# The opening of a hybrid attention and DeltaNet layer: modulation products in plain float32 on four column groups, tokens loaded first, squares shared between two engines

## The chip, the cores and the metric

The kernel runs on one NeuronCore of a Trainium2 chip. The metric is the device time of one execution in microseconds. The core has five engines that each work through their own list in order: TensorE (PE in the profile, with its weight loads PEld), VectorE (DVE), ScalarE (ACT), GpSimd (POOL) and SyncE (SP). In this kernel SP does nothing but issue DMA transfers.

## The reference, cut to what matters

One layer mixes 512 latent tokens x and 256 context tokens ctx, each 1024 wide. Everything starts with a modulation: two vectors c and c_ctx give shifts, scales and gates, and the tokens are normed, scaled and shifted before the first projection.

```python
mod_lat = jax.nn.silu(c) @ w_mod + b_mod          # 1024 -> 6144
mod_ctx = jax.nn.silu(c_ctx) @ w_mod + b_mod
sh1, sc1, g1, sh2, sc2, g2 = ... split(mod_lat, 6)
csh1, csc1, ... = split(mod_ctx, 6)
hx = rms_norm(x) * (1.0 + sc1) + sh1
hc = rms_norm(ctx) * (1.0 + csc1) + csh1
... = split_cols(hx @ w_in)                       # attention q, k, v, DeltaNet q, k, v, gates
... = split_cols(hc @ (w_in[:, :CTX_COLS]))
```

After that come grouped-query attention, a bidirectional gated DeltaNet, a gated merge, an output projection and a gated MLP with a short convolution. The change touches only the part that makes sh1, sc1, csh1, csc1 (the first 2048 columns of w_mod), the norms, hx and hc.

## The kernel before, in words

All matrices are float32. A large product is made from two parts of each operand, a high part in the type float32r and the rest (`split`: a copy on ACT, a subtraction on DVE), and three products high x high, high x low, low x high (`mm3`). A product of plain float32 operands appears in the trace as two matmul instructions.

The opening has these pieces, written out as a list of steps in the string `ORD` (L40) that `step` (L580 and after) executes one by one. The order of TensorE's instructions in this part is pinned to that list; the other engines' orders are chosen by a planner from priorities (`sooner`, `first`) and expected ready times.

- Loads. The string `LORD` (L55) gives the order on the SP queue: `x0` is the context (256 tokens), `x1` and `x2` the latent tokens, `w0` to `w7` are the eight halves of the first 2048 columns of w_mod, each 1 MB, `h0` and `h1` the weights of the first two DeltaNet key heads, 0.5 MB each. Tokens and w halves share `WB` (L56) buffers. Behind them on the queue come the rotary tables and the first key weights.
- Norm (L486 to L492). For each of the three token tiles, ACT squares the two groups of 128 tokens with a running sum, the inverse root is one DVE, one POOL instruction, and DVE scales the tokens in place.
- `x0` to `x11` in `ORD` (`x_cols`). Four float32 transposes each, into one of two PSUM banks, and a copy out by ACT or DVE: after twelve of them the tokens stand with channels on partitions.
- `g`, or `a` and `b` for the two halves (`gemv`, L496). One chunk of the modulation: 1024 channels in eight pieces k of 128, times 512 columns (256 of the shift, 256 of the scale), for the two vectors. The weights stream, the vectors are stationary. For the first `FKS` pieces the weights are split by ACT and DVE and multiplied in float32r with both parts of the vectors (four stationary columns), the rest are plain float32 products with two stationary columns. One PSUM bank (`PMB`), and a copy to `mrow` by ACT.
- `m` (`mod_cols`). Four transposes turn the row into columns, and DVE adds the bias and the two partial rows.
- `y` (`modulate`). For two of the eight channel tiles: scale and shift on DVE (latent) and ACT (context), then the split into the operands hxH, hxL, hcH, hcL.
- `p` (`early_proj`), or its halves `q` and `r` for one head each: one channel tile of the first two key heads' projections. It needs `y` of that tile.
- `d` (`warm`): products of zeros that only keep TensorE busy, four for each unit.

After `p7` the kernel goes on with the attention's keys, whose first product is the group `pq<-whi,hcH` in the trace. It does not return to this part.

Of the kernel before, what the change touches and what calls it, by code (L numbers as in the profile page):

```python
# [14 lines left out]
P = 128  # L15
D = 1024
KT = 8
# [17 lines left out]
POOLW = 0  # L35
ND, D0U = 4, 6
KV = 10
GN = ''
FKS = '4466'
# [6 lines left out]
WHB = 3  # L46
PMB = 1
XV, YV = 4, 0
NS = 2
# [29 lines left out]
def hybrid_layer_body(tc, x, ctxt, xT, consts, cols, rows, w_mod1, w_mod2, w_av, w_aq, w_cm, w_pa, w_pd, w_out,  # L79
                      w_up, w_down, outT, dbg=None):  # L80
    nc = tc.nc
    V, A, G, SP = nc.vector, nc.scalar, nc.gpsimd, nc.sync
# [11 lines left out]
    T = Ordered()  # L94
# [14 lines left out]
    def put(i):  # L109
        return tc.keep_in_program_order(i) if strict[0] else i  # L110
# [6 lines left out]
    def tt(out, a, b, op, eng=None):  # L117
        put((eng or V).tensor_tensor(out=out, in0=a, in1=b, op=op))  # L118

    def ts(out, a, s1, op0, s2=None, op1=None, eng=None):  # L120
        if op1 is None:
            (eng or V).tensor_scalar(out=out, in0=a, scalar1=s1, scalar2=None, op0=op0)
        else:
            (eng or V).tensor_scalar(out=out, in0=a, scalar1=s1, scalar2=s2, op0=op0, op1=op1)  # L124
# [4 lines left out]
    def act(out, a, f=AF.Copy, **kw):  # L129
        put(A.activation(out, a, f, **kw))  # L130

    def split(hi, lo, src):
        act(hi, src)
        tt(lo, src, hi, ALU.subtract)
# [6 lines left out]
    def mm(ps, a, b, start=True, stop=True):  # L141
        T.matmul(ps, a, b, start=start, stop=stop)

    with es:
# [23 lines left out]
        ident = cst[:, C_ID:C_ID + 128]  # L168
# [37 lines left out]
        def xbank():  # L206
            return xps.tile([P, 4, P], F32, name="xb", tag="x")
# [44 lines left out]
        hxH = hxp.tile([P, KT, NL], F32R, name="hxH")  # L252
# [191 lines left out]
        with m1_es:  # L444
            m1 = m1_es.enter_context(tc.tile_pool(name="m1", bufs=1))
            mps = m1_es.enter_context(tc.tile_pool(name="mps", bufs=NB, space=PSUM))
            xs = []
            wms = []

            def ordered_load(out, in_):  # L450
                i = SP.dma_start(out, in_)
                if LPIN:
                    tc.keep_in_program_order(i)

            hw = []
            for op in LORD.split():
                i = int(op[1])
                with sooner():
                    if op[0] == "w":
                        wms.append(m1.tile([P, 4, 512], F32, name="wm", tag="in", bufs=WB))  # L460
                        ordered_load(wms[i], w_mod1[i // 2, i % 2])
# [16 lines left out]
            cs = m1.tile([P, 16], F32, name="cs")  # L478
            act(cs, col[:, S_C:S_C + 16], AF.Tanh, scale=0.5)
            stt(cs, cs, 1.0, col[:, S_C:S_C + 16], ALU.add, ALU.mult)  # L480
            ts(cs, cs, 0.5, ALU.mult)
            cs4 = m1.tile([P, KT, 4], F32R, name="cs4")
            split(cs4[:, :, 0:2], cs4[:, :, 2:4], cs.rearrange("p (k two) -> p k two", two=2))
            ss = m1.tile([P, 6], F32, name="ss")
            rs = m1.tile([P, 6], F32, name="rs")
            for i in range(3):  # L486
                for t in range(2):
                    act(hxH[:, 6:8, :].rearrange("p a b -> p (a b)"), xs[i][:, t, :], AF.Square, accum_out=ss[:, 2 * i + t:2 * i + t + 1])
                sl = slice(2 * i, 2 * i + 2)
                rsqrt(rs[:, sl], ss[:, sl], 1.0 / D, EPS)  # L490
                for t in range(2):
                    ts(xs[i][:, t, :], xs[i][:, t, :], rs[:, 2 * i + t:2 * i + t + 1], ALU.mult)  # L492
            m2 = lambda t, o: t[:, o:o + 16].rearrange("p (s k) -> p s k", s=2)
            wsl = lambda k: slice(k * P, k * P + P)

            def gemv(nb, k0=0, k1=KT):  # L496
                if k0 == 0:
                    mpm[nb] = mps.tile([P, 512], F32, name="pm", tag="pm", bufs=PMB)[0:4]
                ps = mpm[nb]
                for k in range(k0, k1):  # L500
                    wm, j = wms[2 * nb + k // 4], k % 2
                    if k >= int(FKS[nb]):
                        mm(ps[0:2], cs[:, 2 * k:2 * k + 2], wm[:, k % 4, :], False, k == KT - 1)
                        continue
                    if j == 0:
                        wmh = m1.tile([P, 2, 512], F32R, name="wmh", tag="wmh", bufs=WHB)
                        wml = m1.tile([P, 2, 512], F32R, name="wml", tag="wml", bufs=WHB)
                        act(wmh, wm[:, k % 4:k % 4 + 2, :])
                        tt(wml, wm[:, k % 4:k % 4 + 2, :], wmh, ALU.subtract, G if k % 4 == 0 and str(nb) in GN else V)
                    mm(ps, cs4[:, k, :], wmh[:, j, :], k == 0, False)  # L510
                    mm(ps[0:2], cs4[:, k, 0:2], wml[:, j, :], False, k == KT - 1)
                if k1 == KT:
                    mrows[nb] = m1.tile([4, 512], F32, name="mrow", tag="mrow", bufs=2)
# [12 lines left out]
            sides = ((hxH, hxL, mod, hx_pair), (hcH, hcL, modc, hc_pair))  # L526
            stash = [[pair(F32) for _ in range(KT // 2)] for pair in (hx_pair, hc_pair)]
# [42 lines left out]
            mrows, mpm = {}, {}  # L570
# [32 lines left out]

            for op in ORD.split():
                step(op[0], int(op[1:]))
# [81 lines left out]
        with kv_es:  # L687
# [716 lines left out]
        for p in range(NP):  # L1404
# [7 lines left out]
            out = (None, gdn_out(0), gdn_out(1), gdn_reload())[p]  # L1412
# [12 lines left out]
        x1 = [x1p.tile([P, NL], F32, name=f"x1_{c}") for c in range(KT)]  # L1425
# [258 lines left out]
```

## Time and profile before

| what | value |
|---|---|
| device time, median of 3 runs | 1252.84 us (1252.52 to 1253.11) |
| span of the profiled execution, first to last instruction | 1246.8 us |
| time of the profiled execution outside its span | not listed on the page; the median above is 6.0 us over the span |
| TensorE busy | 1194.3 us, 96% of the span |
| VectorE, ScalarE, GpSimd busy | 828.6, 613.8, 248.8 us |
| TensorE's mean granted clock | 0.985 |

The profile has these views. The page gives busy times and the costliest groups. The timeline gives one engine's instructions in order: start, length, engine, line, operation, `output<-inputs`, and in brackets how long the engine sat idle before it and what released it. Instructions on a tile have the tile's name without its number, and where a helper records an operation, all have the helper's line (L87 for products, L91 for transposes, L118, L122, L124, L127 for DVE and POOL operations, L130 for ACT). The table of stages gives each engine's busy time and number of instructions between two times, then the granted clock, the DMA share and the rate in GB/s. A length on TensorE includes the pipeline's end, so the distance of two starts is what an instruction occupies.

### The profile page before, as it was taken

To read this page: it belongs to the slowest core of one execution; us is meant where nothing else is said; L and a number is where in the kernel's file an instruction comes from. 1 tells how busy PE (TensorE), PEld (TensorE's weight loads), DVE (VectorE), ACT (ScalarE), POOL (GpSimd) and SP (SyncE) were. 2 spreads that over 40 slices of the span, in tenths; PEclk is the share of its full clock that TensorE was granted. 3 is DMA by queue.
4 is the path that set the end of the run, shared out by engine and by line. 5 is a ranking of instruction groups with operands and counts; after the bars stand their busy time and mean duration, and the time that the engine had idled before them with its cause. 6 is when DMAs were issued, how large, how long until landed. Compare 5 with 4: busy or idle time off the path is not lost.

```text
span 1246.8 us, 20481 instructions
## 1 busy us (share of the span) xinstructions
PE 1194.3 (96%) x7733; PEld 1018.2 (82%) x7733; DVE 828.6 (66%) x1623; ACT 613.8 (49%) x1403; POOL 248.8 (20%) x333
## 2 busy tenths in 40 slices
PE   7999999999999989999999999999999999999996
PEld 4599889888887778788887778789888888888886
DVE  5766767878699757666646687866766755653333
ACT  6634467777565754754634532234544444442321
POOL 0120110010313596596483000000000000000000
PEclk8999999999999999999999999999999999999998
DMA  9412321333536526345335685863344323323331
GB/s 380 144 60 85 92 80 60 119 98 106 199 104 211 165 73 189 111 153 176 118 123 186 225 273 196 302 235 114 103 135 135 125 95 102 101 82 104 93 94 68
DMA packets 67555, 174.98 MB, mean 140 GB/s; under 512 B 7456, under 2 KB 18176, under 8 KB 66048
## 3 DMA queue, kind: packets, MB, share of 16 engines
q1 hardware_dynamic: 67456, 173.67, 41.9%
q8 instruction: 61, 1.00, 0.3%
q14 instruction: 38, 0.31, 0.1%
HBM read 146.85 MB, written 26.79 MB: 139 GB/s over the span
## 4 chain that ended last, share of the span: by engine, by line
PE 52%; DMA 4%; DVE 3%; ACT 2%; POOL 1%; issue 1%; SPq 0%; POOLq 0%; DVEq 0%; ACTq 0%
PE mc L87 33%; PE mb L87 13%; PE pb L87 5%; DMA gt<-atd 1%; DVE wlo L118 1%; DMA M<-gamdr 1%; ACT whi L130 1%; PE pk L87 1%; DMA wl<-in_w_mod_dram 1%; PE pqk L87 0%; POOL NN L118 0%; DMA wraw<-in_w_pa_dram 0%; DMA cw<-in_rows_dram 0%; DMA NN<-gamdr 0%; ACT Gb L130 0%
## 5 line engine op out<-in xcount | busy, mean ns | idle before, releaser
L118 DVE TENSOR_TENSOR wlo<-wraw,whi 128x1024 fp32r<-128x1024 f32 (+1 forms) x153 | 188.0, 1230 | 158.2 <-ACT whi L130 157.7
L130 ACT ACTIVATE whi<-wraw 128x1024 fp32r<-128x1024 f32 (+1 forms) x153 | 159.6, 1044 | 217.0 <-PE mc L87 114.4
L87 PE MATMUL mc<-h,whi 128*128 128x512 f32 (+1 forms) x752 | 219.6, 376 | 0.3 <-ACT whi L130 0.3
L87 PE MATMUL mb<-hxH,whi 128*128 128x512 f32 x384 | 162.3, 423 | 1.7 <-DVE t L127 1.7
L87 PEld LDWEIGHTS mc<-h,whi 128*128 128x128 f32 x752 | 138.0, 188 | 25.8 <-ACT whi L130 0.5
L87 PE MATMUL mb<-hxH,wlo 128*128 128x512 f32 x384 | 152.3, 397 | 0.0
L87 PE MATMUL mb<-hxL,whi 128*128 128x512 f32 x384 | 152.0, 396 | 0.0
L87 PE MATMUL mc<-h,wlo 128*128 128x512 f32 (+1 forms) x376 | 141.3, 376 | 0.5 <-DVE wlo L118 0.5
L87 PE MATMUL mc<-a,whi 128*128 128x512 f32 (+1 forms) x396 | 111.0, 366 | 0.6 <-DVE x L127 0.6
L118 POOL TENSOR_TENSOR rc<-rc,mhalf 128x2 f32<-128x2 f32 x4 | 3.2, 810 | 456.0 <-DVE rc L124 456.0
L87 PEld LDWEIGHTS mb<-hxH,wlo 128*128 128x128 f32 x384 | 73.0, 190 | 16.8
L87 PEld LDWEIGHTS mb<-hxH,whi 128*128 128x128 f32 x384 | 73.4, 191 | 11.9 <-issue 2.1
L87 PEld LDWEIGHTS mc<-h,wlo 128*128 128x128 f32 x376 | 70.8, 188 | 13.8 <-DVE wlo L118 1.0
L87 PEld LDWEIGHTS mc<-a,whi 128*128 128x128 f32 x396 | 71.6, 189 | 12.8 <-DVE x L127 0.8
L87 PEld LDWEIGHTS mb<-hxL,whi 128*128 128x128 f32 x384 | 73.4, 191 | 9.2
L87 PE MATMUL mc<-a,wlo 128*128 128x512 f32 (+1 forms) x198 | 72.3, 365 | 0.0
L127 DVE SCALAR_TENSOR_TENSOR u<-mc,col,u 128x511 f32<-128x511 f32 x88 | 65.3, 746 | 1.4
L118 POOL TENSOR_TENSOR R<-R,prod 128x31 f32<-128x31 f32 (+15 forms) x93 | 58.0, 623 | 6.7
L118 POOL TENSOR_TENSOR prod<-X,R 128x31 f32<-128x31 f32 (+15 forms) x93 | 53.2, 572 | 20.0 <-DVE X L118 13.2
L87 PE MATMUL pq<-whi,hxH 128*128 128x256 f32 (+1 forms) x192 | 55.5, 289 | 0.0
L87 PE MATMUL pq<-wlo,hxH 128*128 128x256 f32 (+1 forms) x192 | 54.3, 283 | 0.1
L87 PE MATMUL pq<-whi,hxL 128*128 128x256 f32 (+1 forms) x192 | 54.2, 282 | 0.0
(329 smaller groups left out, 2737.5 us busy)
## 6 DMA issues: line engine op xcount, KB each, us to landing
wraw<-in_w_cm_dram SPq DMA_DIRECT2D x48, 512.0 KB, 3.6
wraw<-in_w_up_dram SPq DMA_DIRECT2D x44, 512.0 KB, 3.3
wl<-in_w_mod_dram SPq DMA_DIRECT2D x24, 512.0 KB, 4.9
wm<-in_w_mod_dram SPq DMA_DIRECT2D x8, 1024.0 KB, 10.5
wraw<-in_w_down_dram SPq DMA_DIRECT2D x16, 512.0 KB, 3.6
wraw<-in_w_aq_dram SPq DMA_DIRECT2D x10, 512.0 KB, 3.8
M<-gamdr SPq DMA_DIRECT2D x64, 64.0 KB, 4.5
wraw<-in_w_pa_dram SPq DMA_DIRECT2D x8, 512.0 KB, 4.5
```

Of the source, the lines that this page charges most:

```text
L87: i = nc.tensor.matmul(*a, **k)
L118: put((eng or V).tensor_tensor(out=out, in0=a, in1=b, op=op))
L127: V.scalar_tensor_tensor(out=out, in0=a, scalar=s, in1=b, op0=op0, op1=op1)
L130: put(A.activation(out, a, f, **kw))
```

## The change

- `LORD`: the three token tiles are loaded first, then w0, w1, h0, h1, and the other w halves. `WB` goes from 6 to 8 buffers.
- The norm: ACT squares the first group of each token tile and DVE the second.
- `gemv`: no split of the weights. The two vectors stand in a stationary operand of 32 columns, 30 of them zero (`cs32`, cleared by POOL). Piece k is a plain float32 product that writes the 32 PSUM partitions of column group k modulo 4, so that a half (four pieces) addresses the four groups of the array one after another. `mrow` has 128 partitions.
- `mod_cols`: instead of transposes, four float32 products with 128 columns of `mrow` stationary and a selector `sel` (128 x 2) streaming; the selector adds the four groups' rows of each vector. DVE has one addition per vector instead of two.
- `ORD`: all products in halves; the first chunk now comes among and behind the transposes, and one warming step stands before the first turn into columns.

```diff
-ORD = 'd4 g0 x0 x1 x2 x3 m0 x4 x5 x6 x7 x8 a1 x9 x10 x11 y0 b1 p0 m1 y1 p1 g2 p2 m2 y2 p3 g3 q4 m3 y3 r4 p5 p6 p7'
+ORD = 'd4 x0 x1 x2 x3 x4 x5 x6 x7 a0 x8 x9 x10 x11 b0 d1 m0 y0 a1 p0 b1 p1 m1 y1 a2 b2 p2 m2 y2 p3 a3 b3 p4 m3 y3 p5 p6 p7'
...
-LORD = 'w0 w1 x0 x1 x2 w2 w3 h0 h1 w4 w5 w6 w7'
-WB = 6
+LORD = 'x0 x1 x2 w0 w1 h0 h1 w2 w3 w4 w5 w6 w7'
+WB = 8
...
-            ts(cs, cs, 0.5, ALU.mult)
-            cs4 = m1.tile([P, KT, 4], F32R, name="cs4")
-            split(cs4[:, :, 0:2], cs4[:, :, 2:4], cs.rearrange("p (k two) -> p k two", two=2))
+            cs32 = m1.tile([P, KT, 32], F32, name="cs32")
+            G.memset(cs32, 0.0)
+            ts(cs32[:, :, 0:2], cs.rearrange("p (k two) -> p k two", two=2), 0.5, ALU.mult)
+            sel = m1.tile([P, 2], F32, name="sel")
+            V.tensor_reduce(out=sel, in_=ident.rearrange("p (b c) -> p c b", c=32)[:, 0:2, :], axis=AX.X, op=ALU.add)
...
-                for t in range(2):
-                    act(hxH[:, 6:8, :].rearrange("p a b -> p (a b)"), xs[i][:, t, :], AF.Square, accum_out=ss[:, 2 * i + t:2 * i + t + 1])
+                junk = [hxH[:, k:k + 2, :].rearrange("p a b -> p (a b)") for k in (6, 2)]
+                act(junk[0], xs[i][:, 0, :], AF.Square, accum_out=ss[:, 2 * i:2 * i + 1])
+                V.scalar_tensor_tensor(out=junk[1], in0=xs[i][:, 1, :], scalar=1.0, in1=xs[i][:, 1, :], op0=ALU.mult, op1=ALU.mult,
+                                       accum_out=ss[:, 2 * i + 1:2 * i + 2])
...
-                    wm, j = wms[2 * nb + k // 4], k % 2
-                    if k >= int(FKS[nb]):
-                        mm(ps[0:2], cs[:, 2 * k:2 * k + 2], wm[:, k % 4, :], False, k == KT - 1)
-                        continue
-                    if j == 0:
-                        wmh = m1.tile([P, 2, 512], F32R, name="wmh", tag="wmh", bufs=WHB)
-                        wml = m1.tile([P, 2, 512], F32R, name="wml", tag="wml", bufs=WHB)
-                        act(wmh, wm[:, k % 4:k % 4 + 2, :])
-                        tt(wml, wm[:, k % 4:k % 4 + 2, :], wmh, ALU.subtract, G if k % 4 == 0 and str(nb) in GN else V)
-                    mm(ps, cs4[:, k, :], wmh[:, j, :], k == 0, False)
-                    mm(ps[0:2], cs4[:, k, 0:2], wml[:, j, :], False, k == KT - 1)
+                    q = slice(32 * (k % 4), 32 * (k % 4) + 32)
+                    mm(ps[q], cs32[:, k, :], wms[2 * nb + k // 4][:, k % 4, :], k < 4, k >= 4)
...
-                pst = xbank()[:, 0, 0:16].rearrange("p (a b) -> p a b", b=4)
+                pst = xbank()[:, 0, 0:8].rearrange("p (a b) -> p a b", b=2)
                 for i in range(4):
-                    T.transpose(pst[:, i, :], mrow[:, i * P:(i + 1) * P], ident[0:4, 0:4])
+                    mm(pst[:, i, :], mrow[:, i * P:(i + 1) * P], sel)
...
                     tt(m2(md, 0)[:, :, ks], p4[:, :, :, j], m2(col, S_BMOD)[:, :, ks], ALU.add)
-                    tt(m2(md, 0)[:, :, ks], p4[:, :, :, 2 + j], m2(md, 0)[:, :, ks], ALU.add)
```

More of the change, by code (lines that the diff above doesn't have):

```diff
@@ L37 @@
 KV = 10
-GN = ''
-FKS = '4466'
-ORD = 'd4 g0 x0 x1 x2 x3 m0 x4 x5 x6 x7 x8 a1 x9 x10 x11 y0 b1 p0 m1 y1 p1 g2 p2 m2 y2 p3 g3 q4 m3 y3 r4 p5 p6 p7'
+ORD = 'd4 x0 x1 x2 x3 x4 x5 x6 x7 a0 x8 x9 x10 x11 b0 d1 m0 y0 a1 p0 b1 p1 m1 y1 a2 b2 p2 m2 y2 p3 a3 b3 p4 m3 y3 p5 p6 p7'
 RK = 1.0
@@ L45 @@
 TG = 1
-WHB = 3
 PMB = 1
@@ L497, in gemv @@
                 if k0 == 0:
-                    mpm[nb] = mps.tile([P, 512], F32, name="pm", tag="pm", bufs=PMB)[0:4]
+                    mpm[nb] = mps.tile([P, 512], F32, name="pm", tag="pm", bufs=PMB)
                 ps = mpm[nb]
                 for k in range(k0, k1):
-                    wm, j = wms[2 * nb + k // 4], k % 2
-                    if k >= int(FKS[nb]):
-                        mm(ps[0:2], cs[:, 2 * k:2 * k + 2], wm[:, k % 4, :], False, k == KT - 1)
-                        continue
-                    if j == 0:
-                        wmh = m1.tile([P, 2, 512], F32R, name="wmh", tag="wmh", bufs=WHB)
-                        wml = m1.tile([P, 2, 512], F32R, name="wml", tag="wml", bufs=WHB)
-                        act(wmh, wm[:, k % 4:k % 4 + 2, :])
-                        tt(wml, wm[:, k % 4:k % 4 + 2, :], wmh, ALU.subtract, G if k % 4 == 0 and str(nb) in GN else V)
-                    mm(ps, cs4[:, k, :], wmh[:, j, :], k == 0, False)
-                    mm(ps[0:2], cs4[:, k, 0:2], wml[:, j, :], False, k == KT - 1)
+                    q = slice(32 * (k % 4), 32 * (k % 4) + 32)
+                    mm(ps[q], cs32[:, k, :], wms[2 * nb + k // 4][:, k % 4, :], k < 4, k >= 4)
                 if k1 == KT:
-                    mrows[nb] = m1.tile([4, 512], F32, name="mrow", tag="mrow", bufs=2)
+                    mrows[nb] = m1.tile([P, 512], F32, name="mrow", tag="mrow", bufs=2)
                     act(mrows[nb], ps)
             def mod_cols(nb, mrow):
-                pst = xbank()[:, 0, 0:16].rearrange("p (a b) -> p a b", b=4)
+                pst = xbank()[:, 0, 0:8].rearrange("p (a b) -> p a b", b=2)
                 for i in range(4):
-                    T.transpose(pst[:, i, :], mrow[:, i * P:(i + 1) * P], ident[0:4, 0:4])
+                    mm(pst[:, i, :], mrow[:, i * P:(i + 1) * P], sel)
                 ks = slice(2 * nb, 2 * nb + 2)
```

## The prediction, made before the result was known

> **What bounds the kernel now.** I read the page first (span, busy shares), then a table of stages, then the opening engine by engine in order of time.
>
> ```profile
> span 1246.8 us, 20481 instructions
> PE 1194.3 (96%) x7733; PEld 1018.2 (82%) x7733; DVE 828.6 (66%) x1623; ACT 613.8 (49%) x1403; POOL 248.8 (20%) x333
> ...
> 23.70:35.90 12.20, 10.35 (x36) 4.65 (x36) 10.97 (x15) 8.93 (x14) 0.00 (x0) 0.72 1.02 421
> 35.90:65.30 29.40, 29.00 (x142) 17.98 (x142) 21.66 (x41) 17.15 (x31) 3.23 (x2) 1.00 0.27 88
> 65.30:150.00 84.70, 84.65 (x707) 84.44 (x706) 58.42 (x210) 35.19 (x132) 11.65 (x11) 1.00 0.24 79
> ```
>
> The columns are length, busy PE, PEld, DVE, ACT, POOL, clock, DMA share, GB/s. From 65.3 us PE is full (84.65 of 84.70) and nothing behind it is changed. So the change is worth what it moves the first key product, at 65.25, and I let the rest follow unchanged. PE is already full from 35.9 (29.00 of 29.40); before that it has holes.
>
> ```profile
> 7.83 0.40 PE L87 MATMUL pm<-wmh,cs 128*4 128x512 f32 x1
> 11.01 3.60 PE L87 MATMUL pm<-wm,cs 128*2 128x512 f32 x8
> 15.85 0.33 PE L91 MATMUL pt<-cst,xs 128*128 128x128 f32 x1 [1.25 <-DVE xs L122]
> 26.92 0.78 PE L87 MATMUL pm<-wmh,cs 128*4 128x512 f32 x1
> 30.48 1.10 PE L91 MATMUL pt<-cst,xs 128*128 128x128 f32 x8
> 32.42 3.59 PE L87 MATMUL pm<-wm,cs 128*2 128x512 f32 x8
> 35.94 0.39 PE L87 MATMUL pc<-hcH,whi 128*128 128x256 f32 x1
> 40.79 0.40 PE L87 MATMUL pm<-wmh,cs 128*4 128x512 f32 x1
> 45.47 0.39 PE L87 MATMUL pc<-hcH,whi 128*128 128x256 f32 x1
> ...
> 56.67 0.41 PE L91 MATMUL xb<-cst,mrow 4*128 4x4 f32 x4
> 57.01 0.38 PE L87 MATMUL pc<-hcH,whi 128*128 128x256 f32 x1
> 60.60 0.38 PE L87 MATMUL pc<-hcH,whi 128*128 128x256 f32 x1 [0.17 <-ACT hcH L130]
> 65.25 0.28 PE L87 MATMUL pq<-whi,hcH 128*128 128x256 f32 x1
> ```
>
> The token transposes run from 15.85 to 32.42, the early projections from 35.94 to 65.25, with two mixed products inside, the third of the four from 40.79 to 45.47, 4.68 us, and the fourth of the same make, and three turns into columns, 0.34 each (56.67 to 57.01). The eight steps of early projections with their small waits are therefore 29.31 - 2 x 4.68 - 3 x 0.34 = 18.9 us, 2.3 a step.
>
> **Part 1: tokens first on the SP queue.** SP issues the same transfers in another order, so it pays nothing.
>
> ```profile
> GB/s 19 243 426 414 442 410 442 414 438 314 404 414 444 422 430 418 418 389 404 188 2 8 0 0 62 228 152 158 64 8 0 0 0 0 0 312 81 0 8 0
> ...
> 6.71 2.01 ACT L130 ACTIVATE wmh<-wm 128x1024 fp32r<-128x1024 f32 x2 [2.14 <-DMA wm<-in_w_mod_dram]
> 11.70 1.06 ACT L130 ACTIVATE hxH<-xs 128x1024 fp32r<-128x1024 f32 x1 [2.98 <-DMA xs<-in_ctxt_dram]
> 12.66 0.19 ACT L130 ACTIVATION_READ_ACCUMULATOR hxH<-xs 128x1 f32 x1
> 14.64 0.59 ACT L130 ACTIVATE mrow<-pm 4x512 f32<-4x512 f32 x1 [0.62 <-PE pm L87]
> ```
>
> The first line is the rate in slices of 2 us. The first megabyte is there at 6.71 and the third at 11.70, 2.5 us each. So the three token tiles land at 6.7, 9.2, 11.7 instead of 11.7, 14.2, 16.7, and the modulation's halves w0 and w1 at 14.2 and 16.7, the two early weights by 19.2, w2 at 21.7, w3 24.2, w4 26.7, and, with 0.26 MB of masks between, w7 near 35. With eight buffers only w5 to w7 wait for a token tile, the last until the transposes end. Behind it on SP stand the rotary tables and the first key weights; they leave no later than now (28.3), and the key stage wants them near 59.
>
> **Part 2: half the squares on DVE.**
>
> ```profile
> 14.06 0.17 DVE L124 TENSOR_SCALAR rs<-ss 128x2 f32<-128x2 f32 x1 [3.89 <-ACT hxH L130]
> 15.04 1.42 DVE L122 TENSOR_SCALAR xs<-xs,rs 128x1024 f32<-128x1024 f32 x2 [0.81 <-POOL rs L118]
> ...
> L397 DVE SCALAR_TENSOR_TENSOR wl<-wl,cw 128x1024 f32<-128x1024 f32 x24 | 29.2, 1218 | 7.6 <-DMA wl<-in_w_mod_dram 7.6
> L397 DVE DVE_READ_ACCUMULATOR wl<-wl,cw 128x1 f32 x24 | 1.9, 81 | 0.0
> ```
>
> A square costs ACT 1.15 (11.70 to 12.85); the nearest DVE form, the same multiply with a sum, 1.22 + 0.08 = 1.30. Both of a tile run together and end at 8.0. The norm takes 0.98 (14.06 to 15.04), so scaling starts at 9.03, and the first transposes 0.81 later (15.04 to 15.85), at 9.85. DVE then has in order: scaling to 10.45, two squares to 13.05, two scalings to 15.9; behind the waiting squares stand only these scalings. Now x0 to x11 take 32.42 - 15.85 less the half product (26.92 to 30.48, 3.56) and the first turn (about 0.4): 12.6, or 1.05 each. Four transposes are 0.55 (1.10 for eight), so half of that is waiting for copies. ACT loses half the squares and the splits there, so I take 1.0 each: 21.9 without a0. From below: last scaling at 15.9 and four tiles at 0.55, x11 over near 18.5 with a0 inside. From above: 1.3 each, 25.5.
>
> **Part 3: the products.** Out go ten ACT copies of 1.05 (two are 2.01) and ten DVE subtractions of about 1.2; PE is full from 35.9 beside them, so they buy nothing there. In come per half four plain float32 products, each two instructions 0.43 apart ((3.59 - 0.59) / 7, the group at 32.42 and its line below): 3.42 in series, 0.86 on four column groups at once. The trace has no product with full rows and a quarter of the columns. The nearest are the products of the solve on tiles differing in rows and columns both.
>
> ```profile
> L87 PE MATMUL pm<-wm,cs x24: 591/592/592, 11.0 to 54.5; 128*2 128x512 f32 x24
> ...
> 403.40:404.36 0.96, 0.92 (x94) 1.00 0.71 285
> ...
> 404.37 0.82 PE L87 MATMUL pk<-kT 128*128 128x128 f32 x5
> ...
> 414.11 0.39 PE L87 MATMUL mb<-hxH,wlo 128*128 128x512 f32 x1
> 414.43 0.92 PE L87 MATMUL pb<-TTm,NN 64*64 64x64 f32 x24
> 415.27 1.16 PE L87 MATMUL pk<-kT 128*128 128x128 f32 x8
> 416.19 0.47 PE L87 MATMUL mb<-hxH,whi 128*128 128x512 f32 x1
> ```
>
> A float32 instruction over 128 columns takes 0.92 / 8 = 0.115 in series, so over 32 columns 0.029, and 94 would be 2.7 us; on four tiles they took 0.93: 2.9 times faster. Two tiles: 24 x 0.0575 = 1.38 against 0.84, 1.6 times. Going into small tiles costs 0.32 instead of 0.23. So a half lies between 0.86 and 3.42, with 3.42 / 2.9 = 1.18 by the nearest row; I take 1.0, the ideal with the switch. In strict order, where a product's second instruction waits for its first and the next group starts only then, a half is 5 x 0.43 = 2.15; the 94 would then take 1.37, and took 0.93.
>
> A rule speaks against all this. The Trainium skill, TensorE: Matmul & The Clock Gate (Part 3, What overlaps and what doesn't), says a weight load overlaps running products only when its row group differs, and here all groups hold the same rows. The same part lists 2.38 times for three column groups, an estimate of 1.4 us a half. No run here shows which holds.
>
> **Part 4: the selector sum.** Four products with 128 stationary columns instead of four small transposes; ACT's copy out of PSUM stays 0.59, since its row length stays 512.
>
> ```profile
> 863.12 0.36 PE L87 MATMUL mc<-cst,sq 128*128 128x1 f32 x2
> 863.34 0.36 PE L87 MATMUL mc<-cst,acc 128*128 128x1 f32 x2
> ```
>
> 0.22 each, 0.9 a turn against 0.34. Two of DVE's four additions go, about 0.2. From the turn to the first projection that needs it: 57.01 to 60.60, 3.6, which I take as 3.4 for the first. The selector, the zeroed weights (POOL has nothing until 14.31) and the small products with 0.5 come before 6.7 and cost nothing.
>
> **Part 5: the clock.**
>
> ```profile
> 20.37:23.79 3.42, 1.38 (x11) 1.00 0.99 408
> 23.79:27.20 3.41, 1.90 (x9) 0.50 1.04 436
> 27.20:30.60 3.40, 3.40 (x10) 0.50 1.01 426
> ```
>
> After 1.38 us of work in 3.42 the clock was halved, and it came back after a full 3.40. In the changed kernel the warming products end at 7.83 and transposes begin at 9.85, so the transposes will run partly at half speed; the pace of 1.0 allows for it, and I give a0 1.5 instead of 1.0. The added warming step of four products (0.9) hides beside the copy of the row.
>
> **The sum.** a0 among the transposes: b0 starts at 21.9 + 1.5 = 23.4, ends 24.4; row copied 25.0; turn 25.9; first projection 25.9 + 3.4 = 29.3 (now 35.94), a1 hidden in that wait, weights long there. Then 18.9 for the projections, five halves 5.0, three turns 2.7, and two waits: p2 stands behind its columns, 3.6 - 2.0 (a2 and b2) = 1.6; p6 has only p5 before it, 3.6 - 2.3 = 1.3. Together 29.5, so the key stage starts at 58.8, where w7 (35) and the key weights have long landed. That is 65.25 - 58.8 = 6.45 us earlier: span 1240.4. The page gives no other time for the profiled execution than its span; the median of the runs, 1252.84, is 6.0 above it, for what lies around, and I keep that: 1246.4 us.
>
> **Rivals.**
> Half clock to the first projection: transposes 0.98 a tile instead of 0.55 push the pace from 1.0 to about 1.15 (+1.8), a0 +0.5, b0 +1.0, warming and turn +1.6: 4.9 later, gain 1.5, 1251.3. For it: the gap after 7.83. Against: one full stretch brings the clock back.
> Strict order, a half of 2.15: seven halves on the path 7 x 1.15, less the 1.6 that a2 and b2 no longer leave idle: +6.4, no change, 1252.8. This is also the point from which the sign turns. Against it the 0.93 above.
> No concurrency at all, so that the change does not do what it says: 7 x 2.42 - 1.6 = 15.3 later, 8.9 slower than now, 1261.7. For it: groups in the same rows are nowhere in the trace.
> Weight loads in the open beside serial products: a load of 0.1, so that a half is 8 x 0.53 = 4.24, and 7 x 3.24 - 1.6 = 21.1 later: 14.6 slower, 1267.4.
> ```profile
> 403.44 0.10 PEld L87 LDWEIGHTS pb<-o_nt,NN 32*32 32x32 f32 x1 [0.88 <-DVE o_nt L1022]
> ```
> The skill's rule on row groups would give this one; the tiles here hide their loads, but they differ in rows.
>
> **How the numbers follow.** Forecast 0.55, half clock 0.10, strict order 0.15, none 0.14, open loads 0.06. The forecast's own range: x11 at 18.5 and 0.86 a half make it about 5 us better, 1241; 1.18 a half (+1.0) and 1.3 a tile (+3.6) worse, 1251. The whole range, 1239 to 1262, leaves out the open loads, half of no concurrency and little below. I call within 0.2% (2.5 us) no change, about what can be told. Faster takes 0.95 of the forecast, 0.4 of the half clock (its 1.5 lies inside the bound) and 0.3 of strict order, which sits on the turning point: 0.52 + 0.04 + 0.045 = 0.61. The same: 0.02 + 0.045 + 0.05 = 0.12. Slower, with both cases without concurrency: 0.27.
>
> **What would show it.** Right: eight starts of the new products within 1 us; first projection near 29; key stage near 59 with waits before p2 and p6 only; transposes from about 10. Wrong: starts 0.43 apart throughout (none) or a half of 2.1 (strict order); half clock beyond 24; a first projection that waits for the scaling or the copies; or a shift at 59 that does not arrive at the end, when a later stage is paced by something else.

## The result and the profile after

The changed kernel takes 1239.49 us in the median of 4 executions (1236.03 to 1241.01), beside 1252.97 (1252.52 to 1254.86) for the kernel before on the same chip: a ratio of 0.9888, 95% interval 0.9871 to 0.9904. A second series of the same two gave 1240.57 (6 executions) against 1251.44 (11), 0.9908 [0.9881, 0.9936]. Over all series the medians are 1252.0 (71 executions of before, standard deviation 2.9, from 1244.5 to 1259.0) and 1240.0 (10 of after): a gain of 12 us, where 6.45 was forecast. The direction and the main mechanism, products that run at once on four column groups, were right; the size forecast was half of what came.

The page of the changed kernel, its busy line, and the table of stages up to its key stage (columns as in the tables of the prediction):

```profile
span 1238.2 us, 20489 instructions
PE 1183.2 (96%) x7753; PEld 1015.6 (82%) x7753; DVE 818.8 (66%) x1611; ACT 601.7 (49%) x1386; POOL 248.3 (20%) x334
...
0.00:56.30 56.30, 47.64 (x261) 32.54 (x262) 31.34 (x66) 28.46 (x52) 3.82 (x13) 0.91 0.74 288
56.30:65.30 9.00, 9.00 (x78) 9.00 (x77) 6.55 (x14) 4.14 (x16) 5.39 (x6) 1.00 0.30 108
```

The profiled execution took 1239.93 us, so 1.7 lie outside its span. In the 9.00 us in which the kernel before still worked on projections, this one is already in the key stage with a full TensorE. TensorE's timeline shows the opening step by step:

```profile
1.49 5.33 PE L84 MATMUL pt<-hxH 128*128 128x512 f32 x16 [1.49 <-DVE hxH L563]
9.80 0.33 PE L88 MATMUL pt<-cst,xs 128*128 128x128 f32 x1 [2.98 <-DVE xs L119]
17.87 1.16 PE L84 MATMUL pm<-wm,cs 128*32 128x512 f32 x8
18.96 1.13 PE L88 MATMUL pt<-cst,xs 128*128 128x128 f32 x8
21.45 1.06 PE L84 MATMUL pm<-wm,cs 128*32 128x512 f32 x8
22.45 1.20 PE L84 MATMUL pt<-hxH 128*128 128x512 f32 x4
23.65 1.05 PE L84 MATMUL xb<-sel,mrow 128*128 128x2 f32 x8
24.63 1.06 PE L84 MATMUL pm<-wm,cs 128*32 128x512 f32 x8
27.04 0.38 PE L84 MATMUL pc<-hcH,whi 128*128 128x256 f32 x1 [1.34 <-ACT hcH L127]
37.96 0.38 PE L84 MATMUL pc<-hcH,whi 128*128 128x256 f32 x1 [0.48 <-ACT hcH L127]
43.88 1.92 PE L84 MATMUL pm<-wm,cs 128*32 128x512 f32 x16
45.74 0.39 PE L84 MATMUL pc<-hcH,whi 128*128 128x256 f32 x1
51.60 0.38 PE L84 MATMUL pc<-hcL,whi 128*128 128x256 f32 x1 [0.37 <-DVE hcL L115]
56.28 0.28 PE L84 MATMUL pq<-whi,hcH 128*128 128x256 f32 x1
```

The reader is to see four things. Sixteen instructions of two halves start at 43.88 and the next work at 45.74: 0.93 a half, where one product after the other would take 3.4. The first projection stands at 27.04 instead of 35.94, and the key stage at 56.28 instead of 65.25: 8.97 us earlier. From the first projection on the only idle times left are one inside it (0.37 at 27.79), two at p2 (0.48 at 37.96 and one of 0.37) and two in p6 (0.37 at 51.60 and one of 0.21). And the rest passes the shift on: from the key stage to the end it is 1238.2 - 56.28 = 1181.9, before 1246.8 - 65.25 = 1181.6.

### The profile page after: what moved, and what is told of

Read it like the earlier page. It is cut to its first block, busy times and chain, and to the rows that moved or that the text cites. A ratio compares the mean times of both kernels' runs of the same rounds, so it can differ in the third digit from the quotient of the medians.

```text
span 1238.2 us, 20489 instructions
## 1 busy us (share of the span) xinstructions
PE 1183.2 (96%) x7753; PEld 1015.6 (82%) x7753; DVE 818.8 (66%) x1611; ACT 601.7 (49%) x1386; POOL 248.3 (20%) x334
## 4 chain that ended last, share of the span: by engine, by line
PE 53%; DMA 4%; DVE 4%; ACT 2%; issue 1%; POOL 1%; SPq 0%; POOLq 0%; DVEq 0%; ACTq 0%
PE mc L84 33%; PE mb L84 13%; PE pb L84 5%; DMA gt<-atd 1%; DVE wlo L115 1%; DMA M<-gamdr 1%; PE pk L84 1%; ACT whi L127 0%; DMA wl<-in_w_mod_dram 0%; PE pqk L84 0%; DMA sz<-gdr 0%; POOL NN L115 0%; DMA cw<-in_rows_dram 0%; DMA Gb<-gamdr 0%; DMA NN<-gamdr 0%
## 5 line engine op out<-in xcount | busy, mean ns | idle before, releaser
L84 PEld LDWEIGHTS mc<-a,whi 128*128 128x128 f32 x396 | 71.5, 189 | 12.9 <-DVE x L124 0.8
L124 DVE SCALAR_TENSOR_TENSOR u<-mc,col,u 128x511 f32<-128x511 f32 x88 | 65.3, 746 | 1.4
```

Of the source, the lines that this page charges most:

```text
L84: i = nc.tensor.matmul(*a, **k)
L124: V.scalar_tensor_tensor(out=out, in0=a, scalar=s, in1=b, op0=op0, op1=op1)
```

## The experiments

The columns of this table come from the profile of each run (key stage: start of the first `pq<-whi,hcH`) and from its executions.

| run | key stage | first projection | span | median of the executions (number) | ratio to before [95%] |
|---|---|---|---|---|---|
| e1_before | 65.24 | 34.78 | 1248.0 | 1252.44 (12) | 1.0007 [0.9987, 1.0028] |
| e10_before_look | 65.41 | 34.95 | 1249.0 | 1250.85 (1) | |
| e11_before_look | 64.32 | 33.52 | 1250.0 | 1251.82 (1) | |
| e6_after_again | 56.84 | 27.53 | 1239.3 | 1240.57 (6) | 0.9908 [0.9881, 0.9936] |
| e2_one_group | 72.96 | 33.66 | 1252.8 | 1255.68 (10) | 1.0026 [1.0008, 1.0045] |
| e9_two_groups | 59.26 | 27.74 | 1241.9 | 1243.79 (1) | |
| e3_products_only | 56.55 | 31.08 | 1239.8 | 1242.30 (4) | 0.9911 [0.9885, 0.9936] |
| e7_products_again | 56.67 | 31.34 | 1237.9 | 1238.85 (5) | 0.9895 [0.9868, 0.9923] |
| e4_loads_squares | 79.63 | 38.01 | 1260.9 | 1262.66 (5) | 1.0075 [1.0047, 1.0103] |
| e5_squares_act | 57.13 | 27.99 | 1236.9 | 1238.08 (4) | 0.9893 [0.9866, 0.9920] |
| e8_warm | 54.13 | 26.99 | 1234.8 | 1237.54 (5) | 0.9895 [0.9869, 0.9921] |
| e14_warm_again | 55.69 | 28.76 | 1238.7 | 1239.14 (6) | 0.9900 [0.9881, 0.9919] |
| e12_before_late | 75.17 | 36.13 | 1259.2 | 1259.65 (6) | 1.0061 [1.0041, 1.0082] |
| e13_after_late | 64.56 | 26.91 | 1246.0 | 1246.43 (12) | 0.9965 [0.9948, 0.9983] |

### Do the column groups work at once?

The theory is that four groups run concurrently and a half costs about 1.0; the rivals are a strict order (2.15) and no concurrency (3.42). In e2_one_group all eight products of a chunk go to the first group, and the row and the selector have 32 partitions. In e9_two_groups two groups take turns.

```diff
 # e2_one_group
-                    mm(ps[q], cs32[:, k, :], wms[2 * nb + k // 4][:, k % 4, :], k < 4, k >= 4)
+                    mm(ps[0:32], cs32[:, k, :], wms[2 * nb + k // 4][:, k % 4, :], k == 0, k == KT - 1)
...
 # e9_two_groups
-                    q = slice(32 * (k % 4), 32 * (k % 4) + 32)
-                    mm(ps[q], cs32[:, k, :], wms[2 * nb + k // 4][:, k % 4, :], k < 4, k >= 4)
+                    q = slice(32 * (k % 2), 32 * (k % 2) + 32)
+                    mm(ps[q], cs32[:, k, :], wms[2 * nb + k // 4][:, k % 4, :], k < 2, k >= 6)
...
```

> The changed kernel, with all eight products of a chunk on the first column group one after another (32 partitions out, the selector over 32 rows). Theory 1: the four groups run at once and are worth 3.42 - 0.93 = 2.49 us a half; b0 starts and ends 5 us later, five more halves follow the first projection, about 2.2 of waiting is filled: the key stage at 56.3 + 15.2 = 71.5, time 15 us over the changed kernel, slower than before. Theory 2: the products on one group overlap as well, or hide beside other waits, and the groups are worth less than 5 us; then the gain came from the order of the loads.

> The changed kernel with a chunk's pieces on two column groups in turn instead of four. Theory 1: the groups run at once without limit, so a half takes 2 x 2 x 0.43 = 1.72 and the key stage starts near 56.3 + 7 x 0.79 - about 1.5 of waits filled = 60. Theory 2: strict order with one instruction of overlap: two groups then cost as much as four, 5 x 0.43 = 2.15; the 0.93 measured with four speaks against it: 62 to 63.

TensorE's timeline of e2_one_group, two halves and what follows them:

```profile
42.79 7.05 PE L84 MATMUL pm<-wm,cs 128*32 128x512 f32 x16
...
49.77 0.39 PE L84 MATMUL pc<-hcH,whi 128*128 128x256 f32 x1
...
72.96 0.28 PE L84 MATMUL pq<-whi,hcH 128*128 128x256 f32 x1
```

The same of e9_two_groups:

```profile
35.80 3.63 PE L84 MATMUL pm<-wm,cs 128*32 128x512 f32 x16
39.36 0.38 PE L84 MATMUL pc<-hcH,whi 128*128 128x256 f32 x1
...
59.26 0.28 PE L84 MATMUL pq<-whi,hcH 128*128 128x256 f32 x1
```

From start to start a half takes (49.77 - 42.79) / 2 = 3.49 on one group, (39.36 - 35.80) / 2 = 1.78 on two and 0.93 on four. That is 2.0 and 3.75 times faster. With one group the key stage slides to 72.96, 16.7 us behind after's, and the median to 1255.68, 3.4 over the 1252.3 of before in its series. So the concurrency is what carries the change: without it, it would be a loss. In a strict order two groups would cost what four cost, 2.15; that falls by 1.78 and by 0.93. Both forecasts came close: 71.5 for the key stage of e2_one_group, 60 for that of e9_two_groups, a single execution.

The weight loads can be seen as well. Two rows of after's loads (PEld) beside the sixteen products that start at 43.88:

```profile
43.88 0.16 PEld L84 LDWEIGHTS pm<-wm,cs 128*32 128x32 f32 x8 [0.36 <-issue]
44.34 0.13 PEld L84 LDWEIGHTS pm<-wm,cs 128*32 128x32 f32 x4 [0.30 <-issue]
```

Eight loads are done 0.16 us after the first product has started, and four more come together 0.46 after that start, while products on the same rows stream.

### Which of the parts earns the gain?

e3_products_only is the kernel before with the new products, the zeroed stationary operand and the selector alone; the loads, their buffers, the squares and the order of steps stay those of before. e4_loads_squares is the reverse: loads, shared squares and order of after, with the split products and six buffers of before. e5_squares_act is after with all squares back on ACT.

```diff
 # e3_products_only, and again e7_products_again: before, with after's gemv, mrow and mod_cols; kept from before:
 ORD = 'd4 g0 x0 x1 x2 x3 m0 x4 x5 x6 x7 x8 a1 x9 x10 x11 y0 b1 p0 m1 y1 p1 g2 p2 m2 y2 p3 g3 q4 m3 y3 r4 p5 p6 p7'
 LORD = 'w0 w1 x0 x1 x2 w2 w3 h0 h1 w4 w5 w6 w7'
 # e4_loads_squares: before, with (and with after's squares)
+ORD = 'd4 x0 x1 x2 x3 x4 x5 x6 x7 a0 x8 x9 x10 x11 b0 d1 m0 y0 a1 p0 b1 p1 m1 y1 a2 b2 p2 m2 y2 p3 a3 b3 p4 m3 y3 p5 p6 p7'
+LORD = 'x0 x1 x2 w0 w1 h0 h1 w2 w3 w4 w5 w6 w7'
 # e5_squares_act: after, with
+                for t in range(2):
+                    act(hxH[:, 6:8, :].rearrange("p a b -> p (a b)"), xs[i][:, t, :], AF.Square, accum_out=ss[:, 2 * i + t:2 * i + t + 1])
```

> The kernel before with only the new products and the selector sum; loads, buffers, squares and the written order of steps as before. Theory 1: the products carry most of the gain: half a product less before the first projection (b1, 2.6) and 2 x 2.8 after it, less 3 x 0.6 for the turns: the key stage at 58 to 60, 6 to 7 us below before. Theory 2: the tokens' early landing carries it: the key stage at 62 or later, under 3.5 us below before.

> The changed kernel's order of loads, squares and steps with the products of before (weights split for float32r); six buffers instead of eight, since the split weights need the room. Theory 1: without the short products the new order gains nothing: b0 is about 5 us later and the later halves cost what they did, the key stage at 64 to 69, time within 4 us of before. Theory 2: the early tokens alone bring 4 us or more: the key stage at 61 or earlier.

> The changed kernel with all squares on ACT, as before. Theory 1: a tile's second square comes 1.2 us later, but the twelve transposes are paced by their copies; the key stage is 0 to 1.5 us later, time within 2 us of the changed kernel. Theory 2: the squares on ACT delay the copies as well, six of them 3.6 us, and the key stage starts 3 us later or more.

> The kernel before with only the new products and the selector sum, again, now beside the changed kernel. Its key stage started at 56.55, the changed kernel's at 56.28. Theory 1: the order of loads, the shared squares and the new order of steps are worth nothing on top of the products: within 1.5 us of the changed kernel. Theory 2: they are worth 2 us or more behind the opening: 2 to 4 us over the changed kernel.

The products alone bring the key stage to 56.55 and 56.67, within 0.4 of after's 56.28 and 56.84, and the time to 1242.30 and 1238.85, on both sides of after's. That is more than theory 1 gave them (58 to 60). TensorE's timeline of e3_products_only:

```profile
27.16 1.06 PE L84 MATMUL pm<-wm,cs 128*32 128x512 f32 x8
30.08 1.06 PE L84 MATMUL pm<-wm,cs 128*32 128x512 f32 x8
31.08 0.39 PE L84 MATMUL pc<-hcH,whi 128*128 128x256 f32 x1
```

Its first projection comes 4 us later than in after, at 31.08, but from there it needs 56.55 - 31.08 = 25.5 instead of 56.28 - 27.04 = 29.2. The rows account for 3.2 of these 3.8 us. The half b1 (0.93) lies before the first projection here and behind it in after. In after a halved stretch of the clock, 1.7 us lost, falls behind the first projection; here the clock is 1.00 from 31.1 on. And after's idle times from there on add up to 1.8, against a single one of 1.22 here, at 52.35. Tokens first move the first projection forward and win nothing at the key stage. With the old products the same loads and order cost 14 us at the key stage and 10 in the time (e4_loads_squares), more than either theory had. TensorE waits for the split weights and then for ACT:

```profile
20.43 0.39 PE L87 MATMUL pm<-wml,cs 128*2 128x512 f32 x1 [1.87 <-DVE wml L118]
...
38.01 0.58 PE L87 MATMUL pc<-hcH,whi 128*128 128x256 f32 x1 [5.16 <-ACT hcH L130]
```

Ahead of that hcH, ACT made two copies of the modulation's split (1.06 at 31.73, 1.04 at 33.21) and two of the next weights' (1.99 at 35.66). But only 2 to 3 of the 14 us lie before the first projection (38.01, before 35.94). Behind it e4_loads_squares needs 41.6 us instead of 29.3: b1 is done there (3.5, ahead of it in before), further waits of 0.9 to 1.5 add up to 4.5, and two stretches at half clock (to 42.3 and from 56.0 to 62.8) lose 5.6. What the six buffers have to do with it was not tested.

The shared squares do what the prediction said, and it does not matter. The squares of the first tile start together in after, on ACT and on DVE:

```profile
6.67 1.06 ACT L127 ACTIVATE hxH<-xs 128x1024 fp32r<-128x1024 f32 x1 [2.29 <-DMA xs<-in_ctxt_dram]
...
6.67 1.23 DVE L488 SCALAR_TENSOR_TENSOR hxH<-xs 128x1024 fp32r<-128x1024 f32 x1 [1.79 <-DMA xs<-in_ctxt_dram]
```

All on ACT (e5_squares_act), the first transpose waits until 11.19 instead of 9.80:

```profile
11.19 0.33 PE L88 MATMUL pt<-cst,xs 128*128 128x128 f32 x1 [4.24 <-DVE xs L119]
```

but of these 1.39 us only 0.3 to 0.85 are left at the key stage (57.13 against 56.84 and 56.28), and the time, 1238.08, is not above after's.

### What do the halved clocks cost?

In after, the clock was halved twice in the opening. The table of stages:

```profile
11.30:14.70 3.40, 3.04 (x14) 2.25 (x12) 2.48 (x6) 2.69 (x6) 0.70 (x1) 0.50 1.00 424
14.70:18.10 3.40, 3.40 (x18) 2.37 (x20) 2.25 (x6) 0.99 (x3) 0.70 (x1) 0.50 1.01 414
...
24.90:28.40 3.50, 1.79 (x13) 0.76 (x6) 2.73 (x8) 2.75 (x6) 0.00 (x0) 0.99 1.02 414
28.40:31.80 3.40, 3.40 (x13) 2.12 (x15) 0.28 (x1) 0.00 (x0) 0.00 (x0) 0.51 1.01 417
```

The first one, 6.8 us long, lies over the transposes; the second one follows the 1.79 us of work in 3.50 while the first projection waits, and falls on the first projection step, p0, and the start of b1. e8_warm moves the zeros into these two idle places; e14_warm_again is the same kernel once more.

```diff
-ORD = 'd4 x0 x1 x2 x3 x4 x5 x6 x7 a0 x8 x9 x10 x11 b0 d1 m0 y0 a1 p0 b1 p1 m1 y1 a2 b2 p2 m2 y2 p3 a3 b3 p4 m3 y3 p5 p6 p7'
+ORD = 'd7 x0 x1 x2 x3 x4 x5 x6 x7 a0 x8 x9 x10 x11 b0 m0 y0 a1 d2 p0 b1 p1 m1 y1 a2 b2 p2 m2 y2 p3 a3 b3 p4 m3 y3 p5 p6 p7'
```

> The changed kernel with seven warming steps at the start instead of four, none before the first turn into columns and two behind a1, where TensorE waited 1.34 us for the first projection's operands. Theory 1: the half-clock stretches at 11.3 to 18.1 and 28.4 to 31.8 come from TensorE's gaps before them; filled, the transposes and the first two projections run at full clock, and the key stage starts 2 to 4 us earlier, at 52.5 to 54.5. Theory 2: the transposes are paced by the copies and the scaling, so the full clock buys nothing there: key stage within 1 us of 56.3, or later if the warming delays the first transposes.

> The opening without halved clock (after, with its zeros moved into the idle places) once more, for its time against after's 1240.0. Its key stage stood at 54.13 against 56.28 and 56.84. If the 2.4 us pass through: 1237.6. If the rest takes them back: 1240.

In e8_warm the opening ran at full clock throughout and the key stage came at 54.13. The same kernel did not repeat that. Two neighbouring stretches, first of e8_warm:

```profile
20.80:24.20 3.40, 2.28 (x22) 1.28 (x24) 2.84 (x4) 2.20 (x4) 0.00 (x0) 1.00 1.01 422
24.20:27.60 3.40, 3.40 (x20) 2.01 (x13) 2.62 (x7) 2.75 (x6) 0.00 (x0) 1.00 1.01 414
```

then the same of e14_warm_again:

```profile
20.80:24.20 3.40, 2.28 (x19) 1.20 (x17) 2.98 (x3) 2.40 (x4) 0.00 (x0) 1.00 1.01 422
24.20:27.60 3.40, 3.40 (x13) 1.68 (x14) 2.49 (x7) 2.75 (x6) 0.00 (x0) 0.57 1.02 395
```

Equal work, 2.28 us in 3.40, and the clock stays in the one execution and is halved in the other, whose key stage comes at 55.69. (The halving itself begins at 24.65; the 3.41 us before that hold 2.29 us of work in both.) The eleven executions of both have a median of 1238.8, 1.2 under after's, with a standard deviation of some 2 us in each: the zeros help the opening in the profiles by 0.6 to 2.7, and in the time this can't be told from nothing. The Trainium skill, TensorE: Matmul & The Clock Gate (Part 1, What's actually happening), says that the window by which activity is judged runs freely and does not restart with the kernel. The traces agree: in after the halved stretches begin at 11.30 and 28.35, five times 3.41 apart, in e6_after_again, the same code, at 15.85 and 29.50, four times 3.41 apart, while the two executions' first ones are 4.55 apart. The same page (Why this matters for your kernels) advises no gaps above about 3 us; here the clock was halved behind a stretch whose longest gaps were 1.34 (after) and 1.12 (e14_warm_again), so in this kernel the measurement is stricter than that advice.

### Why is the gain larger than the opening?

The medians differ by 12.0, the key stages by 9.0: five profiles of before put the end of its projections at 65.25, 65.24, 65.41, 64.32 and 66.77 (mean 65.4), three of after at 56.28, 56.84 and 56.16 (56.4). So 3.0 us by the medians come from behind the opening, where nothing is changed (the means of the key stages are good to about 0.5). The profiles show less of it. From the key stage to the end they have 1181.6, 1182.8, 1183.6 and 1185.7 for before and 1184.0 with its start shifted (mean 1183.5); 1181.9, 1182.5, and 1181.4 shifted for after (1181.9). That is 1.6, with single values some 2 us from their means. All eleven profiles of changed kernels lie between 1179.8 and 1183.3, those of e4_loads_squares (1181.3, with the old products) and of e3_products_only (1183.3, with the old loads) too.

First the baseline. e1_before, e10_before_look and e11_before_look are the kernel before once more.

> The kernel before, unchanged, to see its own executions with their spans. The changed kernel's profile gained 8.97 us to the first key product (65.25 to 56.28) and 8.6 in the span, but its median is 13.5 us below the median of before. Theory 1: the profiled execution of before (span 1246.8) was a short one; its other executions have the same 1.7 us outside the span as the changed kernel, so spans near 1251, and a lower granted clock (more stretches at half clock) of about 0.981 to 0.983. Theory 2: the kernel before spends 6.0 us outside its span, and its spans are all near 1246.8 at a clock of 0.984 to 0.985; then the change took 4.3 us from outside the span.

> The kernel before, for another profiled execution. So far its two profiles have spans of 1246.8 and 1248.0, its 50-odd executions a median near 1250.4; the changed kernel gains 8.4 to 9.0 us in the opening and 10 to 13 in the medians. Theory 1: the opening is as in the two profiles (key stage at 65.2 to 65.3), and a longer execution loses its 2 to 4 us behind it, in more stretches at half clock or in waits of the DeltaNet stage. Theory 2: the opening varies, since the context operands wait on DVE while POOL builds the rotary tables (two subtractions took 2.69 us instead of 0.75): key stage at 67 or later in a long execution.

> The same once more, to see whether the key stage stays at 65.2 in all executions of the kernel before (theory 1) or moves by 2 us and more (theory 2).

> The changed kernel, unchanged, beside many executions of the kernel before on one chip. Theory 1: the change gives what its opening shows, 8.97 us to the key stage, and the 13.5 us between the first medians were partly chance, since executions of the kernel before were seen between 1247.8 and 1258.7: median 8 to 10 us under before. Theory 2: something behind the opening is shorter too, or the opening of before is longer in most of its executions than in the two profiled ones: 11 to 14 us under before.

The key stage of before lay between 64.3 and 66.8 in five profiles. So it moves by 2.4 us, as the second theory of e11_before_look had it, but not to the 67 named for long executions: the longest profile without zeros, e11_before_look, has the shortest opening. And with 10.9 us the gain in e6_after_again fell just short of its theory 2, 11 to 14.

In every execution of before and after for which both are listed, the time is 1.7 to 1.9 us above the span (six of the nine of e3_products_only and e7_products_again have 2.3 to 2.4). The profiled execution of before, span 1246.8, must then have taken about 1248.6: it was a short one, 3.4 under the median of the 71.

Then the start. In e12_before_late and e13_after_late nine units of zeros stand behind the last projection, so that both kernels enter the key stage about 8.4 us later (7.9 was expected; in e12_before_late the projections also ended 1.5 later than in before, at 66.77).

```diff
 # both
-ORD = '... p5 p6 p7'
+ORD = '... p5 p6 p7 d9'
```

> Before with 36 warming products of zeros (nine units, each four instructions 0.22 apart at full clock, so 7.9 us) behind the last early projection. Nothing else changes. Key stage 65.25 + 7.9 = 73.1 for every theory. What differs is the stretch behind it, which by the medians of before is 1185.4 (1252.3 less 1.8 around the span less 65.1) and of the changed kernels 1181.5. Theory A, the longer stretch belongs to the kernel before whatever the time at which it starts: median 1260.2. Theory B, it hangs on when the stretch starts (where the checks of the clock fall in it): anything from 1254 to 1260, with another mean granted clock than 0.985. Theory C, it is scatter of executions: between the two, by no more than 1.5 us from A.

> After with the same 36 warming products behind the last early projection, so that its key stage starts at 56.5 + 7.9 = 64.4, within a microsecond of that of before. Theory A, the shorter stretch behind belongs to the changed kernel: 64.4 + 1181.7 + 1.8 = 1247.9, 4.4 under before. Theory B, the starting time decides: the stretch becomes that of before, 1251.6, no difference from before that can be told.

e13_after_late has the zeros and the key stage here, on TensorE's timeline:

```profile
56.16 8.34 PE L84 MATMUL pt<-hxH 128*128 128x512 f32 x36
64.56 0.39 PE L84 MATMUL pq<-whi,hcH 128*128 128x256 f32 x1
```

Its key stage begins 0.8 us before the mean of before's, and it is faster by more than that: 1246.43 against 1251.0 in its series, 0.9965 [0.9948, 0.9983], or 4.6 us (2.1 to 6.5). The two shifted kernels differ by 13.2, the unshifted by 12.0. So the time at which the stretch starts is not the cause, and scatter of the times alone isn't either: less the 0.8, the stretch behind the opening is 3.8 us shorter (1.3 to 5.7, with the key stages taken from the profiles). (The rests named above for the shifted kernels are 1259.2 - 75.17 and 1246.0 - 64.56.)

What it is stays partly open. The planner puts a few instructions behind the opening in another order in after (decay exponentials on ACT, some transposes on DVE), but e2_one_group has the order of before there on both engines, and its rest is 1252.8 - 72.96 = 1179.8, the second shortest of all. So another order isn't needed for it. The clock accounts for a part. Each execution lists its mean granted clock, and those of before group like this:

| mean granted clock | executions of before | mean span |
|---|---|---|
| up to 0.982 | 16 | 1252.8 |
| 0.983 to 0.985 | 24 | 1250.7 |
| from 0.986 | 27 | 1248.1 |

Over these 67 executions the correlation is -0.74 and the slope -0.73 us for each 0.001: a little over half of the variance goes with the clock, that is, with how many 3.4 us stretches were halved, and 2.0 of the 2.9 us of standard deviation remain without it. Behind the key stage the tables of stages show seven such stretches, of 1.7 us lost clock each, in two of four profiles of before and six in the other two, and five and six in two of after. Of the shifted kernels before has six and after seven, and after's stretch is the shorter one all the same. The mean clock over the executions is 0.985 in before and 0.986 in after, worth about 0.7 us by that slope. For the rest of the 3 us no row was found; it stays open.

## Why the prediction was right or wrong

- **TensorE full behind the opening, so the change is worth its shift of the key stage.** Right as the main term: 9.0 of 12.0 us. The assumption that the rest follows unchanged failed by the remaining 3.0 (1.6 by the profiles). It was read off the row from 65.3 to 150; the rows of before behind that one do not show a full TensorE:

```profile
150.00:400.00 250.00, 238.79 (x1527) 211.81 (x1527) 198.76 (x422) 169.22 (x446) 33.69 (x28) 0.98 0.36 119
400.00:800.00 400.00, 378.17 (x3122) 320.21 (x3121) 274.31 (x546) 200.47 (x523) 194.46 (x278) 0.98 0.53 172
```

- **Loads.** Right: the squares of the first two token tiles start at 6.67 and 9.20 (forecast 6.7 and 9.2).
- **First transpose at 9.85.** Measured 9.80.
- **Pace 1.0 a transpose step.** Mis-sized: the last of them ends at 21.45, and with a0 taken out (18.96 - 17.87 = 1.09) twelve steps took 10.56, 0.88 each. That is 1.44 us of the sum, although the clock was halved for 6.8 us in this stretch. The prediction put half of a step down to waiting for copies. In after the waits between the transposes are 0.33, 0.22 and 0.35, less than a microsecond in all. The longest of before was not for ACT but for a copy on DVE, which stood behind a subtraction of the split (TensorE's row, then DVE's):

```profile
25.30 1.97 PE L91 MATMUL pt<-cst,xs 128*128 128x128 f32 x8 [2.69 <-DVE hxL L540]
23.42 1.23 DVE L118 TENSOR_TENSOR wml<-wm,wmh 128x1024 fp32r<-128x1024 f32 x1
24.56 0.68 DVE L540 COPY hxL<-pt 128x512 f32<-128x512 f32 x1
```

  e3_products_only, which drops the splits and keeps the old loads and squares, has 0.94 a step (by the starts of its steps, without m0 and a1), although the clock was halved from 13.2 to 26.8. So the splits on both engines, of which the prediction named only ACT's, are part of it; the rest was not tested.
- **a0 at 1.5.** Mis-sized: 1.09, since the halved clock ended at 18.10, just after its start at 17.87.
- **b0 1.0.** Measured 22.45 - 21.45 = 1.00.
- **The warming step hides beside the copy of the row; the row is copied 0.6 after b0.** The first half is right, the second mis-sized. The zeros end as the copy does: the turn starts 23.65 - 22.45 = 1.20 after b0. In e14_warm_again, which has no zeros there, TensorE waits as long for the copy:

```profile
21.06 1.07 PE L84 MATMUL pm<-wm,cs 128*32 128x512 f32 x8
23.25 1.05 PE L84 MATMUL xb<-sel,mrow 128*128 128x2 f32 x8 [1.12 <-ACT mrow L127]
```

  The prediction took the copy's own length and forgot the time before it: in after it runs from 23.00, half a microsecond behind the last product, because ACT was still splitting a weight of the next products:

```profile
22.06 1.05 ACT L127 ACTIVATE whi<-wraw 128x1024 fp32r<-128x1024 f32 x1
23.00 0.59 ACT L127 ACTIVATE mrow<-pm 128x512 f32<-128x512 f32 x1
```

- **Turn 0.9.** Measured 24.63 - 23.65 = 0.98 here, 0.80 to 0.88 later.
- **3.4 from the turn to the first projection.** Mis-sized: 27.04 - 24.63 = 2.41. It was read off a later stretch of before, where ACT and DVE had another order. There ACT began to scale the context 2.14 us after the turn's end (57.01), behind two copies for the latent tokens; in after it did so 0.43 after it (24.63), first of all (the row of before, then that of after):

```profile
59.15 1.09 ACT L130 ACTIVATE hf<-hcL,modc 128x256 f32<-128x256 f32 x2
25.06 1.09 ACT L127 ACTIVATE hf<-hcL,modc 128x256 f32<-128x256 f32 x2 [1.47 <-DVE modc L115]
```

- **From the first projection to the key stage 29.5.** Measured 29.24, but that is luck: two errors cancel in it. The waits were 0.85 at p2 (forecast 1.6) and 0.58 in p6 (1.3), 1.5 less together, and the halved stretch from 28.4 to 31.8 took back 3.4 x 0.49 = 1.7.
- **A half 1.0, between 0.86 and 3.42.** Right: 0.93. The rivals of strict order, of no concurrency and of open weight loads fall with it. e2_one_group is what no concurrency would have been: 1255.68. The Trainium skill's rule in TensorE: Matmul & The Clock Gate (Part 3, What overlaps and what doesn't), that a load overlaps only into another row group, does not hold for these products. All four groups have the same rows, their loads stand beside running products (the rows from 43.88 above), and together they run 3.75 times faster than one; the 2.38 of its table is for three groups.
- **Half clock to the first projection.** The rival was half true: halved stretches came at 11.3 to 18.1 and 28.4 to 31.8, the second beyond the 24 that was named as a sign of being wrong. It cost little: e8_warm, without them and with its zeros in other places, was 2.2 to 2.7 us earlier at the key stage.
- **The median is 6.0 over the span for what lies around.** Wrong: 1.8 lie around, the rest was a short execution. It did no harm to the difference, since the same 6.0 stood on both sides.

The steps that failed, then, by size. First "I let the rest follow unchanged": behind the opening the changed kernel is about 3 us shorter by the medians, and why stays open. Then the sizes in the opening, whose mechanism held: its forecast gain was 2.5 too small, from the pace 1.44, the wait behind the first turn 1.0, a0 0.41 and 0.26 behind the first projection, less 0.6 for the copy of the row, which came later than forecast. The remaining 1.4 of the 13.35 between the stated median of before and the result are the choice of executions: before's three runs stood 0.8 above the median of all its executions, after's four 0.5 under that of all of after's.

Of the change's own parts, the prediction was also wrong in what it did not ask: whether the new loads and order were needed. They were not; within the scatter the new products alone have the whole gain.

## What to carry to other kernels

A chain of small plain float32 products with few stationary columns can be spread over column groups in the same rows, and the partial rows added by a selector: here that was 3.75 times faster than one group, and plain float32 products also need no operand splits. When a stage has waits on both sides of a product, test each part of a bundle alone: the one that moves an intermediate mark (the first projection, 4 us) may move nothing at the end. And take a baseline from many executions, since one profile of this kernel can lie 3 us from its median, more than most single edits are worth.

## What the runs showed that was not expected

- Executions of one kernel differ, among other things, by the number of stretches of 3.4 us with a halved clock, and identical code with identical work before it (2.28 us in 3.40) met both outcomes.
- The stretch before a halving was not idle: 1.79 of 3.50 us in after, 2.28 of 3.40 in e14_warm_again.
- Four column groups in the same rows scale almost fully: 3.49, 1.78, 0.93 us for eight float32 instructions of 512 elements on one, two and four groups.
- The changed kernel is some 3 to 4 us faster behind its opening, with its start shifted to that of before too (e13_after_late), and the mean clock explains less than one of them.
